# HGRN2 mixer on one Trainium2 core: values projected with positions on the partitions, two heads in a product of 256 columns

## The chip, the cores and the metric

The kernel runs on one core of a Trainium2 chip. The metric is the device time of one execution in microseconds, the median of the runs shown.

## The reference

Two layers of a decoder trunk on 1024 positions of width 1024. Layer 0 mixes with dilated window attention, layer 1 with HGRN2, a gated linear recurrence; each mixer is followed by a squared-ReLU MLP, and each sub-layer by a layer norm. The change is in layer 1's mixer, in short:

```python
q_raw, f_raw, i_raw = jnp.split(x @ w_in, [H * K, 2 * H * K], axis=-1)
log_f = jnp.logaddexp(jnp.log(lb), jnp.log1p(-lb) + jax.nn.log_sigmoid(z))
key = (1.0 - lb) * jax.nn.sigmoid(-z)
q = jax.nn.silu(q_raw); v = i_raw
b = jnp.cumsum(log_f, axis=3)                     # within chunks of 64 positions
q_dec, k_dec = q * jnp.exp(b), key * jnp.exp(-b)
a = jnp.where(causal, q_dec @ k_dec.T, 0.0)
kv = (key * jnp.exp(b_last - b)).T @ v            # per chunk, added up by a scan
o = a @ v + q_dec @ state                         # then RMS norm per head
return o @ w_out
```

There are 8 heads of width 128. The forget input f gives the keys (needs a chain of exponentials, logarithms and a running sum), q the queries, and i the values v, which no function is applied to.

## The kernel before, in words

Every fp32 product of the projections is made of three products in fp32r: each operand is split into a high part (a ScalarE copy, L146) and a low part (a VectorE subtraction, L147), and high x high, high x low and low x high are added up in PSUM. The input x lies transposed in SBUF, with its 1024 features on the partitions in 8 blocks, and the positions in two halves of 512 columns.

The mixer is `hgrn` (L1593). Its loop goes over 8 heads; each head has three projections (t = 1 forget, 0 query, 2 values) of two halves each, six slots. A slot is `proj` (L175 to L184): 24 products of 512 columns, weights stationary (128 x 128), positions moving, into one of three PSUM banks (`mm`), so the result has the head's 128 features on the partitions and positions as columns. ScalarE copies it out (L1755) to the tile ze (forget), qe (query) or vTh (values). After the second half of a forget or query projection `gate` (L1696) runs on all 1024 positions: L1703 to L1720 for the forget chain on ScalarE, VectorE and GpSimd (it makes the keys `kd`, L1716, in the tile called ls, and `kd2`, L1719, in ze), L1725 to L1731 for the query chain (`qd`, in qe). Head 0 is gated in halves, each right after its slot.

The rest of a head is cut into pieces (`head_pieces`, L1602) that are run behind the slots of the heads that follow, one list of pieces a slot (`pend`): first the transposes of the values (8 on TensorE and two ScalarE copies, L1605 to L1612, from vTh to vn, positions on the partitions), the scores (`amat`, L1615, products "as") and the transposes of the keys; then `kv(0)`; `omat(0)` and `kv(1)`; `omat(1)` (products "ho", L1645); nothing; and the output's transposes `otr` (L1675, products "opt"), each with a ScalarE copy to oN that multiplies by the norm's weight (L1680). The last head's pieces are left over and are given to the output projection `outproj_ln` (L932) as `fill`, which spreads them over its own products (`tick`, L964). Before the last slot `pre(oN)` loads and splits the first two tiles of the output weights (woh, wol) and of the heads' outputs (onr to hoh, hol).

SBUF tiles come from a pool of slots of 4 KB per partition (`U`, L102), PSUM from pools of banks (`bank`, L105: 3 mm, 2 s, 2 pt, 1 o). A scheduler that runs when the kernel is built fixes the order of the instructions on every engine from their readiness and the order of the program; on the chip each engine runs its own list in that order, and an instruction that waits holds up all that stand behind it. The weights of the next projections are loaded by SyncE (L152, 512 KB each) and split as a whole (128 x 1024).

Of the kernel before, what the change touches and what calls it, by code (L numbers as in the profile page):

```python
# [12 lines left out]
AF = mybir.ActivationFunctionType  # L13
# [47 lines left out]
       (30, 31, 33, 34, 35, 37, 39, 39, 40, 41, 41, 43, 43, 44))  # L61
STATS = ((13, 14, 16), (22, 23, 25))
# [6 lines left out]
def trunk_kernel(  # L69
# [6 lines left out]
    w_hgrn: bass.AP,  # L76
    w_hgrn_out: bass.AP,
# [1498 lines left out]
    class GateW:  # L1576


        def __init__(self):
            self.order = [(hd, t) for hd in range(8) for t in (1, 0, 2)]  # L1580
            self.loaded, self.raw = {}, None

        def ask(self):
            hd, t = self.order[0]
            self.raw = U("wr")
            nc.sync.dma_start(self.raw, w_hgrn[t * 8 + hd])

        def prefetch(self, i):
            if i < len(self.order) and i not in self.loaded:
                hd, t = self.order[i]  # L1590
                self.loaded[i] = w_load(w_hgrn[t * 8 + hd], "w", self.raw if i == 0 else None)

    def hgrn(xs, late, consts, pre, gw):  # L1593
# [6 lines left out]
        order, loaded, prefetch = gw.order, gw.loaded, gw.prefetch  # L1600

        def head_pieces(hd, kd, kd2, qd, vT, dec, oNt):  # L1602
            st = {}

            def trans(src, name):  # L1605
                d = U(name)
                for j in range(2):
                    pt = bank("pt", "hpt")
                    for i in range(4):
                        b = j * 4 + i  # L1610
                        nc.tensor.transpose(pt[:, i * P:(i + 1) * P], src[:, b * P:(b + 1) * P], ident)
                    act(d[:, j * 512:(j + 1) * 512], pt, AF.Copy)  # L1612
                st[name] = d

            def amat(j):  # L1615
                s = bank("s", "as")
                for i in range(4):
                    t = j * 4 + i
                    nc.tensor.matmul(s[:, i * P:(i + 1) * P], kd[:, t * P:(t + 1) * P], qd[:, t * P:(t + 1) * P],
                                     start=True, stop=True, skip_group_check=True)  # L1620
                nc.vector.copy_predicated(aTs[j], cm, s)

            def kv(j):
# [21 lines left out]
            def omat(j):  # L1645
                o = bank("o" if j == 0 else "s", "ho")
                for i in range(4):
# [27 lines left out]
            def otr(j):  # L1675
# [8 lines left out]
            amats = [lambda: amat(0), lambda: amat(1)]  # L1684
            keys = lambda: trans(kd2, "k2n")
            return [
                [lambda: trans(vT, "vn")] + (amats + [keys] if hd else [keys] + amats),
# [3 lines left out]
                [],  # L1691
# [41 lines left out]
        oN = []  # L1733
        pend = []
        prefetch(0)
        n = 0
        for hd in range(8):
            e = {}
            slots = [(t, h) for t in (1, 0, 2) for h in range(2)]
            if hd == 0:  # L1740
                slots = [(1, 1), (0, 1), (2, 1), (1, 0), (0, 0), (2, 0)]
                for i in range(3):
                    prefetch(i)
            seen = set()
            cur = {}
            for t, h in slots:
                bi = hd * 3 + (1, 0, 2).index(t)
                prefetch(bi)
                prefetch(bi + 1)
                if t not in e:  # L1750
                    e[t] = U(("qe", "ze", "vTh")[t])
                if bi == len(order) - 1 and h == 1 and hd:
                    pre(oN)
                o = proj(loaded[bi], xs[h])
                act(e[t][:, h * 512:(h + 1) * 512], o, AF.Copy)  # L1755
                both = (t, 1 - h) in seen
                seen.add((t, h))
                if pend:
                    for f in pend.pop(0):
                        f()  # L1760
                if late:
                    late.pop(0)()
                if hd == 0 or both:
                    gate(hd, t, e, cur, slice(h * 512, h * 512 + 512) if hd == 0 else slice(0, S))
            for i in range(3):
                del loaded[hd * 3 + i]
            oNt = U("oN")
            oN.append(ond[1, hd] if hd < SPILL[1] else oNt)
            new = head_pieces(hd, cur["kd"], cur["kd2"], cur["qd"], e[2], cur["dec"], oNt)
            if hd == 0:  # L1770
                new = [[]] + new
            pend = [(pend[i] if i < len(pend) else []) + (new[i] if i < len(new) else [])
                    for i in range(max(len(new), len(pend)))]
        return oN, pend
# [59 lines left out]
def _arrays(inputs):  # L1834
# [4 lines left out]
    def cols(w):  # L1839
# [10 lines left out]
        "w_hgrn": cols(i["hgrn_w_in"][0]),  # L1850
# [30 lines left out]
```

## Time and profile before

| | us |
|---|---|
| median of three runs | 2781.69 |
| lowest and highest run | 2781.52, 10449.96 |
| the profiled execution | 2781.63 |
| its span in the trace | 2779.8 |

The trace is of one execution. Its times count from the start of the span. A row of the timeline that ends in "x8" stands for eight instructions that follow one another; its length is from the first one's start to the last one's end. A product in plain fp32, as the scores, is run in two passes, so that eight of the program are sixteen in the trace. In brackets stands how long the engine was idle before a row, and which tile and line it waited for. "ScalarE" is ACT in the rows, "VectorE" DVE, "TensorE" PE, "SyncE" SP (SPq its DMA queue) and "GpSimd" POOL.

### The profile page before, as it was taken

What the parts mean: (1) busy time and instruction counts of PE and PEld (TensorE: products, weight loads), DVE (VectorE), ACT (ScalarE), POOL (GpSimd) and SP (SyncE); (2) the same over time, 40 slices, a digit from 0 to 9 for tenths busy, and PEclk for the clock granted to TensorE, in tenths of its full rate; (3) what the DMA queues carried; (4) which work ended last, traced back from release to release, by engine and by line L of the source; (5) the groups of instructions that cost most, each with busy time, mean ns of one, the idle gap of its engine ahead of it and who ended that gap; (6) DMA issues with size and microseconds to landing.
All of it is one profiled execution on the core that took longest, in us unless ns stands there. A gap on an engine that the chain in (4) does not pass through costs nothing. (4 is left out here: it accounts for less than half of the span.)

```text
span 2779.8 us, 40126 instructions
## 1 busy us (share of the span) xinstructions
PE 2755.9 (99%) x14312; PEld 2230.8 (80%) x14312; DVE 2081.6 (75%) x3880; ACT 1419.2 (51%) x3078; POOL 69.5 (3%) x46
## 2 busy tenths in 40 slices
PE   9999999999999999999999999999999999999998
PEld 7777777777777777888888888888888888888887
DVE  8768777777877779886686868475667887678687
ACT  5555555655555554544454435555553544454443
POOL 0000000000000001000000000110100100000000
PEclk9999999999999999999999999999999999999999
DMA  8766665756656623464493853011132365485654
GB/s 304 251 205 201 193 200 175 245 181 210 203 190 216 187 87 137 159 220 155 166 322 126 265 178 106 11 52 62 61 124 104 139 216 178 142 289 198 215 176 129
DMA packets 204040, 485.01 MB, mean 174 GB/s; under 512 B 28992, under 2 KB 42816, under 8 KB 203840
## 3 DMA queue, kind: packets, MB, share of 16 engines
q1 hardware_dynamic: 202640, 481.99, 51.8%
q8 instruction: 112, 1.84, 0.3%
q14 instruction: 88, 0.72, 0.1%
q10 hardware_dynamic: 1200, 0.46, 0.1%
HBM read 362.69 MB, written 94.11 MB: 164 GB/s over the span
## 5 line engine op out<-in xcount | busy, mean ns | idle before, releaser
L704 PE MATMUL pmm<-xh,H 128*128 128x512 f32 x1008 | 406.9, 404 | 1.4 <-ACT H L466 1.4
L706 PE MATMUL pmm<-xh,H 128*128 128x512 f32 x1008 | 394.4, 391 | 2.4 <-DVE H L474 2.3
L705 PE MATMUL pmm<-xl,H 128*128 128x512 f32 x1008 | 393.4, 390 | 0.9 <-DVE xl L147 0.9
L706 PEld LDWEIGHTS pmm<-xh,H 128*128 128x128 f32 x1008 | 189.2, 188 | 45.9 <-DVE H L474 4.5
L704 PEld LDWEIGHTS pmm<-xh,H 128*128 128x128 f32 x1008 | 189.5, 188 | 41.8 <-issue 3.6
L705 PEld LDWEIGHTS pmm<-xl,H 128*128 128x128 f32 x1008 | 189.8, 188 | 37.0 <-DVE xl L147 1.6
L550 ACT ACTIVATE p<-p,stats 128x128 f32<-128x128 f32 (+1 forms) x384 | 168.2, 440 | 92.3 <-DVE stats L547 92.0
L1355 PE MATMUL pdy<-dT,dS 128*128 128x512 f32 x512 | 199.2, 389 | 0.0
L1358 PE MATMUL pdy<-dT,dS 128*128 128x512 f32 x512 | 199.2, 389 | 0.0
L1359 PE MATMUL pdy<-dT,dS 128*128 128x512 f32 x512 | 199.2, 389 | 0.0
L547 DVE CUSTOM_DVE_ANT_0 p<-s,mask 128x128 f32<-128x128 f32 (+1 forms) x384 | 113.4, 348 | 71.6 <-PE s L536 60.9
L146 ACT ACTIVATE dS<-dr 128x512 fp32r<-128x512 f32 x192 | 119.5, 622 | 76.1 <-PE pdy L1359 34.9
L181 PE MATMUL pmm<-f0nh,wh 128*128 128x512 f32 x384 | 153.2, 399 | 0.0
L183 PE MATMUL pmm<-f0nh,wl 128*128 128x512 f32 x384 | 149.8, 390 | 0.0
L182 PE MATMUL pmm<-f0nl,wh 128*128 128x512 f32 x384 | 149.6, 390 | 0.0
L147 DVE TENSOR_TENSOR dS<-dr,dS 128x512 fp32r<-128x512 f32 x192 | 132.7, 691 | 13.4 <-ACT dS L146 13.3
L146 ACT ACTIVATE dT<-hold 128x512 fp32r<-128x512 f32 x128 | 80.0, 625 | 70.9 <-DVE hold L1334 30.5
L1165 ACT ACTIVATE H<-wc 128x512 fp32r<-128x512 f32 x128 | 77.2, 626 | 76.2 <-DVE wc L1158 48.2
L1358 PEld LDWEIGHTS pdy<-dT,dS 128*128 128x128 f32 x512 | 96.1, 188 | 20.1
L1355 PEld LDWEIGHTS pdy<-dT,dS 128*128 128x128 f32 x512 | 96.1, 188 | 20.0
L1359 PEld LDWEIGHTS pdy<-dT,dS 128*128 128x128 f32 x512 | 96.1, 188 | 19.7
L563 ACT ACTIVATE pts<-ppt 128x256 f32<-128x256 f32 (+1 forms) x192 | 84.6, 474 | 48.9 <-PE ppt L560 46.2
(405 smaller groups left out, 6850.3 us busy)
## 6 DMA issues: line engine op xcount, KB each, us to landing
xh<-xtd SPq DMA_DIRECT2D x110, 512.0 KB
xl<-xtd SPq DMA_DIRECT2D x110, 512.0 KB
dr<-hd SPq DMA_DIRECT2D x192, 256.0 KB
dr<-in_w_down_dram SPq DMA_DIRECT2D x128, 256.0 KB
rot<-e SPq DMA_DIRECT2D x192, 128.0 KB
wa<-in_w_up_dram SPq DMA_DIRECT2D x48, 512.0 KB
wb<-in_w_attn_dram SPq DMA_DIRECT2D x36, 512.0 KB
wa<-in_w_attn_dram SPq DMA_DIRECT2D x33, 512.0 KB
```

The lines of the kernel that those rows point to most:

```text
L146: act(hi, raw, AF.Copy)
L147: nc.vector.tensor_sub(lo, raw, hi.bitcast(F32))
L181: nc.tensor.matmul(o, wh[:, k], xs.h(k), start=k == 0, stop=False)
L182: nc.tensor.matmul(o, wh[:, k], xs.l(k), start=False, stop=False)
L183: nc.tensor.matmul(o, wl[:, k], xs.h(k), start=False, stop=k == NK - 1)
L550: act(p[:, h, :n], p[:, h, :n], AF.Exp, bias=sS[:, 0, h, b:b + 1], scale=-1.0, accum_out=sS[:, 1, h, b:b + 1])
L704: nc.tensor.matmul(o, wh, hi[k // 2][:, c], start=begin and k == 0, stop=False, skip_group_check=True)
L705: nc.tensor.matmul(o, wh, lo[k // 2][:, c], start=False, stop=False, skip_group_check=True)
L706: nc.tensor.matmul(o, wl, hi[k // 2][:, c], start=False, stop=end and k == 3, skip_group_check=True)
L1355: nc.tensor.matmul(o[q], h, T_[:, L], start=begin, stop=False, skip_group_check=True)
L1358: nc.tensor.matmul(o[q], h, T_[:, R], start=False, stop=False, skip_group_check=True)
L1359: nc.tensor.matmul(o[q], l, T_[:, L], start=False, stop=end, skip_group_check=True)
```

## The change

The heads are taken in pairs of 12 slots. Forget and query slots are as before. The values of two heads are projected together, with the roles of the operands exchanged: x is stationary (128 positions), and the weights of two heads, 256 columns, move (`values`). Such a slot makes two blocks of 128 positions, 48 products of 256 columns, and a pair has four of them. The result has positions on the partitions, as `kv` and `omat` want it, so the values are not transposed any more, and the pieces lose that step. The weights of the values come as a new input in this arrangement, in two tiles for each pair.

The order of the slots is now a table (`HORD`, one row for the first pair, one for the others), and so is the slot behind which each piece of the even and the odd head runs (`HPIECE`; 13 is the second slot of the next pair), the slots at which weights are asked for (`HASK`) and given free (`HFREE`). In the later pairs the order is: forget and query of the even head (four slots), three slots of values, forget of the odd head (first half), the last slot of values, query (first half), forget (second half), query (second half). Odd heads, and head 0, are gated in halves, the other even heads as a whole. The last slot of the mixer is thus the second query half of head 7, where before it was the second half of its values. `pre(oN)` is called after that slot's gate; seven lists of head 7's pieces go on to the output projection.

```diff
+HORD = (((1, 0, 1), (0, 0, 1), (2, 4), (1, 0, 0), (0, 0, 0), (2, 6), (2, 0), (2, 2),
+         (1, 1, 0), (0, 1, 0), (1, 1, 1), (0, 1, 1)),
...
+HPIECE = (((7, 8, 9, 10, 11, 12), (13, 14, 15, 16, 17, 18)),
...
-            self.order = [(hd, t) for hd in range(8) for t in (1, 0, 2)]
+            self.aps = []
+            for a in range(0, 8, 2):
+                self.aps += [w_hgrn[8 + a], w_hgrn[a], w_value[a // 2][:, 0:1024], w_value[a // 2][:, 1024:2048],
+                             w_hgrn[8 + a + 1], w_hgrn[a + 1]]
             self.loaded, self.raw = {}, None
...
-        def head_pieces(hd, kd, kd2, qd, vT, dec, oNt):
+        def head_pieces(hd, kd, kd2, qd, vn, dec, oNt):
...
-                                     st["vn"][r, t * P:(t + 1) * P], start=True, stop=True, skip_group_check=True)
+                                     vn(t)[r], start=True, stop=True, skip_group_check=True)
...
-                                         st["vn"][:, t * P:(t + 1) * P], start=True, stop=c == 0,
+                                         vn(t), start=True, stop=c == 0,
...
-            amats = [lambda: amat(0), lambda: amat(1)]
-            keys = lambda: trans(kd2, "k2n")
             return [
-                [lambda: trans(vT, "vn")] + (amats + [keys] if hd else [keys] + amats),
+                [lambda: trans("kd2", "k2n"), lambda: amat(0), lambda: amat(1)],
                 [lambda: kv(0)],
                 [lambda: omat(0), lambda: kv(1)],
                 [lambda: omat(1)],
-                [],
                 [lambda: otr(0)],
                 [lambda: otr(1)],
...
+        def values(n, t0):
+            o = bank("mm", "pmm")
+            w = [loaded[6 * n + 2 + i] for i in range(2)]
+            for i, t in enumerate((t0, t0 + 1)):
+                oc = o[:, i * 256:i * 256 + 256]
+                x_, c = xs[t // 4], slice((t % 4) * P, (t % 4) * P + P)
+                for k in range(NK):
+                    wh, wl = (half[:, (k % 4) * 256:(k % 4) * 256 + 256] for half in w[k // 4])
+                    nc.tensor.matmul(oc, x_.h(k, c), wh, start=k == 0, stop=False, skip_group_check=True)
+                    nc.tensor.matmul(oc, x_.h(k, c), wl, start=False, stop=False, skip_group_check=True)
+                    nc.tensor.matmul(oc, x_.l(k, c), wh, start=False, stop=k == NK - 1, skip_group_check=True)
+            if n not in vals:
+                vals[n] = [U("vn") for _ in range(2)]
+            act(vals[n][t0 // 4][:, (t0 % 4) * 256:(t0 % 4) * 256 + 512], o, AF.Copy)
+        oN, vals = [], {}
...
+        def gates(n, what):
+            if what[0] == 2:
+                return
+            t, b, h = what
+            hd = 2 * n + b
+            if hd == 0 or b:
+                gate(hd, t, *heads[hd], slice(h * 512, h * 512 + 512))
+            elif (hd, t, 1 - h) in done:
+                gate(hd, t, *heads[hd], slice(0, S))
...
+        for i in range(4):
+            prefetch(i)
+        for n in range(4):
+            for i, what in enumerate(HORD[n > 0]):
+                k = 12 * n + i
+                for m in (n - 1, n):
+                    for b in range(2):
+                        if m >= 0 and 12 * m + HPIECE[m > 0][b][0] == k:
+                            begin(m, b, [12 * m + a for a in HPIECE[m > 0][b]])
+                slot(n, what)
+                for j in HFREE[n > 0].get(i, ()):
+                    del loaded[6 * n + j]
+                while todo[k]:
+                    todo[k].pop(0)()
                 if late:
                     late.pop(0)()
+                gates(n, what)
+                if k == 47:
+                    pre(oN)
+                for j in HASK.get(i, ()):
+                    prefetch(6 * n + j)
+        begin(3, 1, [36 + a for a in HPIECE[1][1]])
+        return oN, todo[48:55]
...
-        "w_hgrn": cols(i["hgrn_w_in"][0]),
+        "w_hgrn": cols(i["hgrn_w_in"][0])[:16],
+        "w_value": i["hgrn_w_in"][0][:, 2 * D:].reshape(NK, P, 4, 2 * P).transpose(2, 1, 0, 3).reshape(4, P, NK * 2 * P),
```

On TensorE, at an even head's first pieces in the middle of the mixer, stood in the kernel before (pmm are projections, opt transposes of the output, hpt transposes of values (from vTh) or keys (from ze), as scores):

```order
L183 MATMUL pmm<-f0nh,wl 128x512
L1679 MATMUL opt<-ident,on 128x128 x4
L1611 MATMUL hpt<-ident,vTh 128x128 x8
L1619 MATMUL as<-qe,ls 128x128 x8
L1611 MATMUL hpt<-ident,ze 128x128 x8
L181 MATMUL pmm<-f0nh,wh 128x512
```

There now stands:

```order
L1749 MATMUL pmm<-wh,f0nh 128x256
L1750 MATMUL pmm<-wl,f0nh 128x256
L1751 MATMUL pmm<-wh,f0nl 128x256
L1690 MATMUL opt<-ident,on 128x128 x4
L1621 MATMUL hpt<-ident,ze 128x128 x8
L1630 MATMUL as<-qe,ls 128x128 x8
L190 MATMUL pmm<-f0nh,wh 128x512
```

The eight transposes from vTh are gone, the products ahead have 256 columns with x (f0nh, f0nl) as the stationary operand, and the transposes of the keys come before the scores.

On TensorE, at the end of the mixer, from the last projection's product to the output projection's first (pmm from woh and wol), stood:

```order
L183 MATMUL pmm<-f0nh,wl 128x512
L1679 MATMUL opt<-ident,on 128x128 x8
L1611 MATMUL hpt<-ident,vTh 128x128 x4
L1619 MATMUL as<-qe,ls 128x128 x8
L193 MATMUL pmm<-woh,hoh 128x512
L194 MATMUL pmm<-wol,hoh 128x512
```

There now stands (ho is `omat`):

```order
L192 MATMUL pmm<-f0nh,wl 128x512
L1690 MATMUL opt<-ident,on 128x128 x4
L1621 MATMUL hpt<-ident,ze 128x128
L1690 MATMUL opt<-ident,on 128x128 x4
L1621 MATMUL hpt<-ident,ze 128x128 x3
L1630 MATMUL as<-qe,ls 128x128 x4
L1663 MATMUL ho<-vn,aT 64x128 x2
L1621 MATMUL hpt<-ident,ze 128x128 x4
L1630 MATMUL as<-qe,ls 128x128 x4
L202 MATMUL pmm<-woh,hoh 128x512
L203 MATMUL pmm<-wol,hoh 128x512
```

Key transposes and scores of head 7's second half, which need both of its gates, now stand ahead of the output projection, which follows the last query slot directly.

On ScalarE, at the same place, stood (vTh are copies of the last two values' slots, the a tile is the query gate's work, woh and hoh are splits for the output projection):

```order
L1755 ACTIVATE vTh<-pmm 128x512
L1730 ACTIVATE a_18802<-a_18802 128x1024
L146 ACTIVATE woh<-wor 128x512 x2
L1755 ACTIVATE vTh<-pmm 128x512
L146 ACTIVATE woh<-wor 128x512 x2
L146 ACTIVATE hoh<-onr 128x512 x2
```

There now stands, from just behind the copy of the last query slot (a_18994, ls, ze and dec are steps of the forget gate, a_19135 of the query gate, oN copies of head 6's output):

```order
L1728 ACTIVATE dec<-a_18994 128x8
L1733 ACTIVATE a_19135<-qe 128x512
L1724 ACTIVATE ls<-ze,hc_C 128x512
L1734 ACTIVATE a_19135<-a_19135 128x512
L1691 ACTIVATE oN<-opt,hg 128x512
L1735 ACTIVATE a_19135<-a_19135,one 128x512
L1727 ACTIVATE ze<-ze,hc_C 128x512
L155 ACTIVATE woh<-wor 128x512 x2
L1738 ACTIVATE a_19135<-a_19135 128x512
L155 ACTIVATE woh<-wor 128x512
L155 ACTIVATE hoh<-onr 128x512 x2
```

The splits for the output projection now stand behind the steps of both gates of head 7's second half.

## Rows read from the trace of the kernel before

**Rows 1.** Page: the span, then each engine's busy time, share and instructions.

```profile
span 2779.8 us, 40126 instructions
...
PE 2755.9 (99%) x14312; PEld 2230.8 (80%) x14312; DVE 2081.6 (75%) x3880; ACT 1419.2 (51%) x3078; POOL 69.5 (3%) x46
```

**Rows 2.** Windows: the mixer's stage (stretch, its length, then the columns named).

```profile
core 0: us, PE busy (x) PEld busy (x) DVE busy (x) ACT busy (x) POOL busy (x), PEclk, DMA share, GB/s
1708.60:2053.60 345.00, 344.73 (x2116) 287.27 (x2115) 214.44 (x332) 192.32 (x287) 39.02 (x18) 1.00 0.18 62
```

**Rows 3.** Groups by line, 1708.6 to 2100: busy us, mean ns | idle before.

```profile
L181 PE MATMUL pmm<-f0nh,wh 128*128 128x512 f32 x384 | 153.2, 399 | 0.0
...
L1612 ACT ACTIVATE vn<-hpt 128x512 f32<-128x512 f32 x16 | 8.8, 602 | 0.3 <-PE hpt L1611 0.3
...
L1611 PE MATMUL hpt<-ident,vTh 128*128 128x128 f32 x64 | 8.7, 273 | 0.0
```

**Rows 4.** Timeline, TensorE, a projection: start us, length us, engine, line, operation.

```profile
1799.80 0.39 PE L181 MATMUL pmm<-f0nh,wh 128*128 128x512 f32 x1
...
1802.30 0.39 PE L183 MATMUL pmm<-f0nh,wl 128*128 128x512 f32 x1
```

**Rows 5.** Timeline, TensorE, head 0's transposes (hpt) and scores (as).

```profile
1754.38 1.03 PE L1611 MATMUL hpt<-ident,vTh 128*128 128x128 f32 x8
1755.25 0.39 PE L1619 MATMUL as<-qe,ls 128*128 128x128 f32 x2
1755.72 1.15 PE L1611 MATMUL hpt<-ident,ze 128*128 128x128 f32 x8
1756.70 1.73 PE L1619 MATMUL as<-qe,ls 128*128 128x128 f32 x14
```

**Rows 6.** Timeline, TensorE, attention: scores of 256 columns on 64 partitions.

```profile
303.34 1.14 PE L536 MATMUL s<-kT,qT 64*128 64x256 f32 x8
```

**Rows 7.** Timeline, SyncE's queue at the mixer's start.

```profile
1703.90 1.25 SPq L152 DMA_DIRECT2D wr<-in_w_hgrn_dram  x2
...
1715.65 2.44 SPq L152 DMA_DIRECT2D wr<-in_w_hgrn_dram  x4
```

**Rows 8.** Timeline, ScalarE, the first weight's split, and what it waited for.

```profile
1709.69 1.06 ACT L146 ACTIVATE wh<-wr 128x1024 fp32r<-128x1024 f32 x1 [2.66 <-DMA wr<-in_w_hgrn_dram]
```

**Rows 9.** Timeline, ScalarE, head 0's gates in halves (ze forget, qe query).

```profile
1732.91 0.59 ACT L1755 ACTIVATE ze<-pmm 128x512 f32<-128x512 f32 x1
...
1738.26 0.60 ACT L1755 ACTIVATE qe<-pmm 128x512 f32<-128x512 f32 x1 [0.40 <-PE pmm L183]
...
1746.51 0.71 ACT L1719 ACTIVATE ze<-ze,hc_C 128x512 f32<-128x512 f32 x1
```

**Rows 10.** Timeline, VectorE, the last step of that query gate.

```profile
1746.16 0.69 DVE L1731 TENSOR_TENSOR qe<-qe,a 128x512 f32<-128x512 f32 x1
```

**Rows 11.** Timeline, TensorE, the mixer's last two slots and its end.

```profile
2037.17 0.39 PE L183 MATMUL pmm<-f0nh,wl 128*128 128x512 f32 x1
...
2039.38 0.50 PE L181 MATMUL pmm<-f0nh,wh 128*128 128x512 f32 x1
...
2050.40 1.04 PE L1679 MATMUL opt<-ident,on 128*128 128x128 f32 x8
...
2053.42 0.48 PE L193 MATMUL pmm<-woh,hoh 128*128 128x512 f32 x1
...
2055.37 0.50 PE L195 MATMUL pmm<-woh,hol 128*128 128x512 f32 x1 [0.54 <-DVE hol L147]
```

**Rows 12.** Timeline, ScalarE, splits (woh, hoh) and output copies at that end.

```profile
2051.39 1.14 ACT L146 ACTIVATE woh<-wor 128x512 fp32r<-128x512 f32 x2
2052.44 1.14 ACT L146 ACTIVATE hoh<-onr 128x512 fp32r<-128x512 f32 x2
2053.47 1.25 ACT L1680 ACTIVATE oN<-opt,hg 128x512 f32<-128x512 f32 x2
```

**Rows 13.** Timeline, VectorE, the low part of the output projection's input.

```profile
2054.62 1.29 DVE L147 TENSOR_TENSOR hol<-onr,hoh 128x512 fp32r<-128x512 f32 x2
```

More of the change, by code (lines that the diff above doesn't have):

```diff
@@ L61 @@
        (30, 31, 33, 34, 35, 37, 39, 39, 40, 41, 41, 43, 43, 44))
+HORD = (((1, 0, 1), (0, 0, 1), (2, 4), (1, 0, 0), (0, 0, 0), (2, 6), (2, 0), (2, 2),
[3 rows of a table added]
+HPIECE = (((7, 8, 9, 10, 11, 12), (13, 14, 15, 16, 17, 18)),
+          ((6, 7, 9, 10, 11, 12), (13, 14, 15, 16, 17, 18)))
+HASK = {0: (2,), 1: (3,), 4: (4,), 6: (5,), 8: (6,), 10: (7,)}
+HFREE = ({3: (0,), 4: (1,), 7: (2, 3), 10: (4,), 11: (5,)}, {1: (0,), 3: (1,), 8: (2, 3), 10: (4,), 11: (5,)})
 STATS = ((13, 14, 16), (22, 23, 25))
@@ L76, in trunk_kernel @@
     w_hgrn: bass.AP,
+    w_value: bass.AP,
     w_hgrn_out: bass.AP,
@@ L1579, in __init__ @@
         def __init__(self):
-            self.order = [(hd, t) for hd in range(8) for t in (1, 0, 2)]
+            self.aps = []
+            for a in range(0, 8, 2):
+                self.aps += [w_hgrn[8 + a], w_hgrn[a], w_value[a // 2][:, 0:1024], w_value[a // 2][:, 1024:2048],
+                             w_hgrn[8 + a + 1], w_hgrn[a + 1]]
             self.loaded, self.raw = {}, None
         def ask(self):
-            hd, t = self.order[0]
             self.raw = U("wr")
-            nc.sync.dma_start(self.raw, w_hgrn[t * 8 + hd])
+            nc.sync.dma_start(self.raw, self.aps[0])
         def prefetch(self, i):
-            if i < len(self.order) and i not in self.loaded:
-                hd, t = self.order[i]
-                self.loaded[i] = w_load(w_hgrn[t * 8 + hd], "w", self.raw if i == 0 else None)
+            if i < len(self.aps) and i not in self.loaded:
+                self.loaded[i] = w_load(self.aps[i], "w", self.raw if i == 0 else None)
     def hgrn(xs, late, consts, pre, gw):
@@ L1599, in hgrn @@
         nc.sync.dma_start(sm, smask)
-        order, loaded, prefetch = gw.order, gw.loaded, gw.prefetch
-        def head_pieces(hd, kd, kd2, qd, vT, dec, oNt):
-            st = {}
+        loaded, prefetch = gw.loaded, gw.prefetch
+        def head_pieces(hd, kd, kd2, qd, vn, dec, oNt):
+            st = {"kd": kd, "kd2": kd2}
             def trans(src, name):
-                d = U(name)
+                d, src = U(name), st.pop(src)
                 for j in range(2):
@@ L1616, in amat @@
                 s = bank("s", "as")
+                kd = st["kd"] if j == 0 else st.pop("kd")
                 for i in range(4):
@@ L1731, in gate @@
                 nc.vector.tensor_mul(q, q, a3)
[L1733 to L1760, printed above, removed]
+        def values(n, t0):
[12 more added lines that the diff above has]
+            act(vals[n][t0 // 4][:, (t0 % 4) * 256:(t0 % 4) * 256 + 512], o, AF.Copy)
@@ new lines, in hgrn, with slot @@
+        oN, vals = [], {}
+        todo = [[] for _ in range(64)]
+        heads = [({}, {}) for _ in range(8)]
+        done = set()
+        def slot(n, what):
+            if what[0] == 2:
+                values(n, what[1])
+                return
+            t, b, h = what
+            hd = 2 * n + b
+            e, cur = heads[hd]
+            if t not in e:
+                e[t] = U(("qe", "ze")[t])
+            o = proj(loaded[6 * n + 4 * b + 1 - t], xs[h])
+            act(e[t][:, h * 512:(h + 1) * 512], o, AF.Copy)
+            done.add((hd, t, h))
@@ new lines, in gates, with begin, vn @@
+        def gates(n, what):
+            if what[0] == 2:
+                return
+            t, b, h = what
+            hd = 2 * n + b
+            if hd == 0 or b:
+                gate(hd, t, *heads[hd], slice(h * 512, h * 512 + 512))
+            elif (hd, t, 1 - h) in done:
+                gate(hd, t, *heads[hd], slice(0, S))
+        def begin(n, b, at):
+            hd = 2 * n + b
+            cur = heads[hd][1]
+            oNt = U("oN")
+            oN.append(ond[1, hd] if hd < SPILL[1] else oNt)
+            def vn(t):
+                return two[t // 4][:, (t % 4) * 256 + b * P:(t % 4) * 256 + b * P + P]
+            two = vals.pop(n) if b else vals[n]
+            heads[hd] = None
+            del cur["a"], cur["a3"]
+            for k, fs in zip(at, head_pieces(hd, cur["kd"], cur["kd2"], cur["qd"], vn, cur["dec"], oNt)):
+                todo[k] += fs
@@ L1761, in hgrn @@
                 if late:
                     late.pop(0)()
[L1763 to L1771, printed above, removed]
@@ L1772, in hgrn @@
-            pend = [(pend[i] if i < len(pend) else []) + (new[i] if i < len(new) else [])
-                    for i in range(max(len(new), len(pend)))]
-        return oN, pend
+                gates(n, what)
[5 more added lines that the diff above has]
+        return oN, todo[48:55]
     def rest(f, *args):
```

2 rows, old and new, of the table HORD are left out of this document.

## The prediction

> **What bounds the kernel now.** I read the page first: TensorE is busy for 2755.9 of 2779.8 us, VectorE for three quarters of it, ScalarE for half [rows 1]. So the time is TensorE's work plus the little that it waits, and the question is what the change does to both. Next I read the windows of the stage that is changed, layer 1's mixer: 344.73 of 345.00 us busy, at a granted clock of 1.00 (the upper of the two levels, 2.4 GHz), with VectorE at 214 and ScalarE at 192 us [rows 2]. Nothing there waits. A saving on ScalarE or VectorE is worth nothing in this stage; a microsecond less on TensorE is worth one, as long as no new wait appears. The groups by line say what TensorE does there: 384 products of 512 columns on each of three lines, of which a third is for the values, and 64 transposes of the values, with 16 copies on ScalarE behind them [rows 3]. A row's mean duration (399 ns) is no price, because products overlap. The price is the distance from one start to the next, read from the timeline: eleven distances in 2.50 us, 227.3 ns for a product of 512 columns [rows 4].
>
> **What it removes.** Eight transposes run from 1754.38 to 1755.25, 0.87 us; eight heads have eight each, so 8 x 0.87 = 7.0 us go. In that place of head 0, TensorE also stopped for the copies that empty the two transpose banks (the two "as" from 1755.25 take until 1755.72, though two cost 0.22), 0.25 us more [rows 5]. Total: -7.2. The 16 copies are 16 x 0.60 = 9.6 us of ScalarE [rows 3], which has 153 us free in the stage [rows 2]: nothing.
>
> **What it changes in the products.** The values' 384 products of 512 columns cost 384 x 0.2273 = 87.3 us. They become 768 of 256 columns, the same number of columns altogether. The stage has no row of 256 columns, so I bound the price. From below: eight products of 256 columns in attention (on 64 partitions, with the weights of 64) last 1.14 us from the first start to the last end, and if the last one takes 0.39 the distance is (1.14 - 0.39) / 7 = 107 ns [rows 6]; 768 x 107 = 82.2, a gain of 5.1. In the middle: half of 227.3 is 113.6, and nothing changes. From above, where the pipeline still works: 107 is what the columns take, so 512 take 214, and the remaining 13.6 ns belong to each product however short; then 120.6, 92.6 us, +5.3. A product of 128 columns with a load of 128 columns before it comes every 112 ns (fourteen scores last 1.73 us and two 0.39; the difference is twelve distances, 1.34 us) [rows 5], so a load of that size fits into 112 ns and is just hidden by 256 columns. I take 116 ns, between 112 and 120.6: 768 x 116 = 89.1, +1.8.
>
> The Trainium skill ("TensorE: Matmul & The Clock Gate", section "Back-to-back issue gap") puts a warm product at its columns over 2.4 plus 2.5 ns: 109.2 ns for 256 columns and 215.8 for 512, by which the term would be +1.0 by the page's own two figures; the trace does not bear out the second (227.3 ns [rows 4]). The Trainium skill (the same page, section "LDWEIGHTS (loading the stationary operand)") makes a load as long as its columns at half the column rate, 106.7 ns for 128 columns, about as long as the 256-column product that has to cover it; this speaks against the change, since the cover goes from twice the load to none to spare. The trace's 112 ns agree with it as a floor [rows 5], and the sum stays as it is.
>
> **What it moves.** First the start. The program now asks for four weight tiles instead of three before the first product. In before two are issued at 1703.90 and the rest from 1715.65, behind a store [rows 7]; a tile is split on ScalarE 5.8 us after its issue (1709.69 against 1703.90) [rows 8]. The fourth, the second half of the values' weights, goes behind the store, at 1715.65, and is split 5.8 us later, at 1721.5. The stage begins at about 1709; two slots of 24 x 0.2273 = 5.45 us, two groups of transposes of the stage before (1.7) and twelve products of the third slot (1.4) come before the first product that needs it: 1723. Cost 0, at most 1.
>
> Even heads keep their distance: their query gate has three slots (16 us) before the keys are transposed, as in before. Odd heads have less. Their last forget slot is the eleventh of twelve and their last query slot the twelfth; their keys and scores follow the second slot of the next pair. They are gated in halves, and a half chain is shown by head 0. Forget: from the copy at 1732.91 to the end of the last exponential at 1746.51 + 0.71 = 1747.22, 14.3 us. Query: from 1738.26 to 1746.16 + 0.69 = 1746.85 on VectorE, 8.6 us [rows 9, 10]. The forget half has three slots and some smaller products, 3 x 5.45 = 16.4, and the pieces of the even head between them (2.0 for output products, 8 transposes at 0.109), 19.3 us in all; the query half has two, 10.9 + 0.9 = 11.8 us. Both fit, the second by 3 us. Cost 0, up to 3 us for each of three odd heads.
>
> **The last odd head has no slots behind it.** In before the mixer ended with a values' product, and head 7's gates were under way for two slots before. TensorE went from the last product (2050.40) through transposes and scores into the output projection at 2053.42, and had to wait only 0.54 us, for the low part of its input at 2055.37, 4.97 us after the last product [rows 11]. Now the last slot is head 7's second query half, the slot before it the second forget half. Call the end of the last product T. The forget chain starts 0.4 us after its slot, which ends 5.45 us of products and one piece of output products (2037.17 to 2039.38, 2.2 us with the breaks [rows 11], less one product's 0.2) before T: T - 7.4 + 0.4 + 14.3 = T + 7.3. The query chain ends at T + 0.4 + 8.6 = T + 9.0, and in ScalarE's row there now stand among its steps two copies of the output (1.25 us for both) and two splits of the output's weights (1.14) [rows 12]; part of this falls into pauses of the chain, so I put it at T + 10.5. The order on TensorE has head 7's second four key transposes and four scores ahead of the first product of the output projection: it can start at T + 11. The split of its input (two copies, 1.14 us [rows 12]) now also stands behind the gate's exponential on ScalarE, and its low part on VectorE behind that (0.65 each [rows 13]): T + 12.5 to T + 13 for the product that waited at T + 4.97 before. TensorE's work up to there is 4.9 us (8 + 8 transposes at 0.109, 16 passes of scores at 0.112, five products at 0.23). So it waits 12.75 - 4.9 = 7.8 us, where it waited 0.54: +7, with bounds 3 (the pauses swallow all that is queued, and the first half's work fills more) and 10 (nothing overlaps). Behind the waiting scores stands the whole output projection, so nothing can be done meanwhile.
>
> **Sum.** -7.2 + 1.8 + 7 + 0 = +1.6 on the profiled execution's 2781.63, which is 1.8 above its span and 0.06 below the median of the runs, 2781.69. Forecast: 2783. A measurement of this kernel tells about 2%, 55.6 us, from no change.
>
> **Rivals.**
> A, the forecast: the gain of the transposes is real and is eaten by the wait at the mixer's end. For it: the two half chains of head 0 and the order of the rows. 2783.
> B: the wait at the end is hidden, since ScalarE and VectorE run emptier in that place than in head 0 (no splits of weights for another head), and the sum is -7.2 + 1.8 = -5.4: 2776. Against it: 11 us of chain can't shrink to 3; at least half of the 7 remains unless the steps run much faster than in head 0 [rows 9].
> C: odd heads are late in each pair. The query half has only 3 us to spare, and in ScalarE's order steps of both gates, copies and splits of two 1024-column weight tiles (1.05 us each) stand between. If each of three pairs loses 3 us: 2783 + 9 = 2792.
> D, slower: the load of the weights is not hidden behind 256 columns. Each product then costs its load and its columns one after the other, 112 + 113.6 = 226 ns, as long as a whole one of 512: 768 x 0.226 = 173.6, +86.3, and with the other terms 2783 - 1.8 + 86.3 = 2867. It decides (2%) from 2837, that is 54 / 768 = 70 ns more per product, 186 ns. For it: 112 ns for load and 128 columns is barely less than 113.6. Against it: in attention products of 256 columns, with loads of their own, come every 107 ns [rows 6].
>
> **How the numbers follow.** A 0.60, B 0.23, C 0.11, D 0.03, and 0.03 for what I don't see. The range goes from 2772 (B with the lower price of the products, 2776 - 4, rounded) to 2795 (C, and the upper price): it leaves out D and the unseen. A, B and C are all within 2%: same 0.95. Slower is D and one of the unseen 0.03, 0.04; faster 0.01.
>
> **What would show it.** In the changed kernel's timeline, the distance between two products of 256 columns: 107 to 121 ns is right, 200 is D. No rows of transposes of the values. In the waits of TensorE after the last projection's product: an idle time of 5 to 9 us ended by VectorE (the query's product) or by the split of the output's input; less than 2 us is B. In the windows of the mixer: TensorE idle below 1 us in the interior, else C. The forecast is wrong if the mixer's stage shrinks by over 8 us, or if products of 256 columns take over 130 ns.

## The result and the profile after

The median of five runs is 2795.6 us (2794.7 to 2797.56), that of the kernel before 2782.0. The ratio is 1.005, with a 95% interval from 1.0034 to 1.0066: half a per cent slower, 0.6 us above the forecast's range and 12.6 above its number. The profiled execution took 2797.56 us.

The page of the changed kernel (columns as in [rows 1]):

```profile
span 2795.8 us, 40855 instructions
...
PE 2758.0 (99%) x14632; PEld 2247.6 (80%) x14632; DVE 2073.8 (74%) x3912; ACT 1421.3 (51%) x3114; POOL 73.3 (3%) x54
```

TensorE is busy for only 2.1 us more than before, and the span is 16.0 us longer. So most of the loss is not work. Its two stages, the mixer and the start of the output projection (columns as in [rows 2]):

```profile
1710.50:2062.00 351.50, 341.94 (x2413) 299.94 (x2412) 200.85 (x356) 188.04 (x310) 40.31 (x24) 0.99 0.17 56
2062.00:2114.00 52.00, 46.29 (x270) 37.58 (x269) 35.95 (x73) 25.25 (x50) 2.54 (x2) 0.93 0.37 116
```

The mixer, which had 0.27 us of idle time in 345, now has 9.56 in 351.5, the stretch behind it 5.7, and in both the granted clock is below 1.00 on average. Who waited for whom, TensorE from 1700 to 2130 (us in total, times, longest):

```profile
engine line waited for: us in total, times, longest us
PE ho L1663 <- DVE stB L1650: 9.6, 4, 3.2
PE as L1630 <- DVE qe L1739: 2.6, 1, 2.6
PE ho L1663 <- ACT oN L1691: 2.1, 1, 2.1
PE hpt L1621 <- ACT ze L1727: 0.8, 1, 0.8
PE pmm L204 <- DVE hol L156: 0.3, 1, 0.3
```

The first line is new and stands in the middle of the mixer: four times the output products of `omat(1)` waited for the state scan. The next four are the end of the mixer. By stretches, read from the starts of products in both timelines:

| stretch | before | after | difference |
|---|---|---|---|
| start of the first projection product | 1709.07 | 1710.50 | +1.4 |
| from there to the start of the last projection product | 341.10 | 351.43 | +10.3 |
| from there to the output projection's last product | 107.33 | 111.60 | +4.3 |
| from there to the last product of the kernel | 613.83 | 613.71 | -0.1 |

The first line is not the change's: among the kernels of this study the stage begins between 1708.80 and 1711.89, and up to there TensorE runs the same products. Of the 1.4 us, 1.2 are there already 60 us after the start of the span, behind a stretch of the changed kernel from 39.0 to 42.4 us at a granted clock of 0.50 that the kernel before does not have.

**The products.** Two rows of the timeline of the changed kernel, in a slot of values (start, length):

```profile
1944.08 0.28 PE L1749 MATMUL pmm<-wh,f0nh 128*128 128x256 f32 x1
...
1945.52 0.28 PE L1749 MATMUL pmm<-wh,f0nh 128*128 128x256 f32 x1
```

Twelve distances in 1.44 us: 120.0 ns for a product of 256 columns, against 227.3 for one of 512 [rows 4]. There are no transposes of values any more.

**The wait in the middle.** VectorE's row around the wait that ends at 1966.08, in the third pair (L1673 is the reduction for the norm of the even head's first half, L1650 the scan of the states, L1736 and L1739 steps of the odd head's query gate, L156 a split of weights):

```profile
1956.24 0.69 DVE L1726 TENSOR_TENSOR ze<-a,ze 128x512 f32<-128x512 f32 x1 [1.91 <-ACT ls L1724]
1959.40 0.69 DVE L1673 TENSOR_REDUCE rms<-sq 128x4 f32<-128x512 f32 x1 [2.46 <-ACT sq L1671]
1960.00 0.34 DVE L1650 SCALAR_TENSOR_TENSOR stB<-stB,dec,kvps 128x128 f32<-128x128 f32 x1
...
1960.33 0.69 DVE L1736 SCALAR_TENSOR_TENSOR a<-qe,a 128x512 f32<-128x512 f32 x1
...
1961.01 0.34 DVE L1650 SCALAR_TENSOR_TENSOR stB<-stB,dec,kvps 128x128 f32<-128x128 f32 x1
...
1962.75 0.35 DVE L1650 SCALAR_TENSOR_TENSOR stB<-stB,dec,kvps 128x128 f32<-128x128 f32 x1
...
1963.09 1.22 DVE L156 TENSOR_TENSOR wl<-wr,wh 128x1024 fp32r<-128x1024 f32 x1
...
1965.08 0.68 DVE L1739 TENSOR_TENSOR qe<-qe,a 128x512 f32<-128x512 f32 x1
1965.68 0.72 DVE L1650 SCALAR_TENSOR_TENSOR stB<-stB,dec,kvps 128x128 f32<-128x128 f32 x2
```

The last products of the state (kvps) had ended at 1957.0. The scan's first step on stB runs at 1960.00, because the reduction stands ahead of it in VectorE's row, and that waited 2.46 us for the squares (sq) from ScalarE. So VectorE stood idle from 1956.93 to 1959.40, with the scan's input there from 1957.0. On ScalarE the squares stood behind steps of the odd head's half gates, though TensorE had finished their input at 1955.9:

```profile
1957.60 0.62 ACT L1733 ACTIVATE a<-qe 128x512 f32<-128x512 f32 x1
1958.25 0.63 ACT L1734 ACTIVATE a<-a 128x512 f32<-128x512 f32 x1
1958.78 0.58 ACT L1671 ACTIVATE sq<-ho 128x512 f32<-128x512 f32 x1
```

Then the scan's seven steps take until 1966.4, with two steps of the query gate, a weight split of 1.22 us and the norm between them. TensorE's last product of the slot ended at 1962.91. In the kernel before the same rows on VectorE were these:

```profile
2031.47 0.69 DVE L1662 TENSOR_REDUCE rms<-sq 128x4 f32<-128x512 f32 x1 [2.76 <-ACT sq L1660]
2032.07 0.34 DVE L1639 SCALAR_TENSOR_TENSOR stB<-stB,dec,kvps 128x128 f32<-128x128 f32 x1
...
2034.82 1.11 DVE L1639 SCALAR_TENSOR_TENSOR stB<-stB,dec,kvps 128x128 f32<-128x128 f32 x3
...
2037.14 0.34 DVE L1639 SCALAR_TENSOR_TENSOR stB<-stB,dec,kvps 128x128 f32<-128x128 f32 x1
```

There the reduction came 0.7 us after its input, the scan took 5.4 us, and its last step ended at 2037.48; `omat(1)` began at 2037.49. But what `omat(1)` waits for is not the last step. In the changed kernel it began at 1966.08, when the sixth of the seven steps had just ended (1966.03) and the seventh was still running (until 1966.40), and so it is at all four waits. In the kernel before, the sixth step (the third of the row "x3") ended at 2035.93: `omat(1)` had 1.5 us of slack. In the changed kernel the scan starts 3.0 us behind the last products of the state, against 0.2 before, and takes 6.0 us to the end of its sixth step, against 3.9. Of these 4.9 us, 1.5 go into the slack and 0.2 into a slot that is that much longer; the other 3.2 are the wait.

**The clock.** Windows of the changed kernel around two of these waits (columns as in [rows 2]):

```profile
1872.00:1878.00 6.00, 4.99 (x35) 4.44 (x36) 2.51 (x6) 1.20 (x2) 0.00 (x0) 0.50 0.00 0
...
1960.00:1966.00 6.00, 2.91 (x13) 2.07 (x11) 6.00 (x16) 4.46 (x8) 1.30 (x1) 1.00 0.00 0
1966.00:1972.00 6.00, 5.92 (x50) 5.04 (x51) 3.20 (x9) 2.46 (x6) 0.00 (x0) 1.00 0.00 0
```

In the wait of 3.17 us from 1869.84 the granted clock falls to 0.50, 1.2 GHz, and it stays there until about 1878.8; products of 512 columns start every 427 ns in that stretch. In the wait of the same length in the third pair, and after it, it stays at 1.00.

**The end.** TensorE's rows from the last projection's product to the output projection (to be read beside [rows 11]):

```profile
2062.16 0.60 PE L1690 MATMUL opt<-ident,on 128*128 128x128 f32 x4
...
2066.60 0.44 PE L1663 MATMUL ho<-vn,aT 128*64 128x128 f32 x4 [2.08 <-ACT oN L1691]
2067.82 0.66 PE L1621 MATMUL hpt<-ident,ze 128*128 128x128 f32 x4 [0.79 <-ACT ze L1727]
2071.03 2.07 PE L1630 MATMUL as<-qe,ls 128*128 128x128 f32 x8 [2.56 <-DVE qe L1739]
2072.76 0.77 PE L202 MATMUL pmm<-woh,hoh 128*128 128x512 f32 x1
```

The chain of waits is nearly the forecast one: a copy of the output behind gate steps on ScalarE (2.08), the forget gate's key (0.79), the query gate (2.56). The forecast had the copies as a delay of the query gate, not as a wait of their own. The output projection starts 10.6 us after the last projection's product, at the lower clock.

### The profile page after: what moved, and what is told of

It reads as the page before. It is cut to its first block, busy times and chain, and to the rows that moved or that the text cites. A ratio compares the mean times of both kernels' runs of the same rounds, so it can differ in the third digit from the quotient of the medians.

```text
span 2795.8 us, 40855 instructions
## 1 busy us (share of the span) xinstructions
PE 2758.0 (99%) x14632; PEld 2247.6 (80%) x14632; DVE 2073.8 (74%) x3912; ACT 1421.3 (51%) x3114; POOL 73.3 (3%) x54
## 5 line engine op out<-in xcount | busy, mean ns | idle before, releaser
L156 DVE TENSOR_TENSOR dS<-dr,dS 128x512 fp32r<-128x512 f32 x192 | 131.1, 683 | 13.7 <-ACT dS L155 13.7
L190 PE MATMUL pmm<-f0nh,wh 128*128 128x512 f32 x256 | 102.3, 400 | 0.0
L191 PE MATMUL pmm<-f0nl,wh 128*128 128x512 f32 x256 | 100.6, 393 | 0.0
L192 PE MATMUL pmm<-f0nh,wl 128*128 128x512 f32 x256 | 100.4, 392 | 0.0
```

Source lines behind the costliest of these rows:

```text
L156: nc.vector.tensor_sub(lo, raw, hi.bitcast(F32))
```

## The experiments

The theory after the result: the waits before `omat(1)` come from the order of VectorE's row, where the scan stands behind a reduction that waits for ScalarE, and ScalarE is behind with half gates. The rivals: the half gates' load as such; another resource. Each run is compared with runs of the kernel before on the same chip. Unless said otherwise, an edit is made to the changed kernel.

**e1_swap: states ahead of the first half's output.**

```diff
-                [lambda: omat(0), lambda: kv(1)],
+                [lambda: kv(1), lambda: omat(0)],
```

> State products (kv(1)) are issued ahead of the first half's output products (omat(0)) in each head's third list; nothing else. Theory 1 (four waits of 9.6 us before the even heads' omat(1) come from VectorE's row, where the state scan stands behind the RMS reduction, which itself waits for ScalarE behind the odd head's half gates): the scan can start about 3 us earlier, each wait falls below 1.2 us, 9.6 us become 3 or less, and the fall of the clock behind the second of them is gone: about 2786. Rival (the scan is late because of the sum of the half gates' steps on VectorE, wherever they stand): the waits stay above 6 us together, 2792 to 2796.

2784.19 us, ratio to the kernel before 1.0007 (0.9997 to 1.0016): 11.4 less than the changed kernel. All four waits are gone, and no window of the mixer has a clock below 1.00. VectorE in the same place:

```profile
1947.47 0.69 DVE L1726 TENSOR_TENSOR ze<-a,ze 128x512 f32<-128x512 f32 x1 [1.91 <-ACT ls L1724]
1948.08 1.49 DVE L1650 SCALAR_TENSOR_TENSOR stB<-stB,dec,kvps 128x128 f32<-128x128 f32 x4
...
1951.77 0.68 DVE L1673 TENSOR_REDUCE rms<-sq 128x4 f32<-128x512 f32 x1
1952.36 0.33 DVE L1650 SCALAR_TENSOR_TENSOR stB<-stB,dec,kvps 128x128 f32<-128x128 f32 x1
...
1954.33 0.34 DVE L1650 SCALAR_TENSOR_TENSOR stB<-stB,dec,kvps 128x128 f32<-128x128 f32 x1
```

The scan's four first steps run at 1948.08 in one piece, 3.7 us ahead of the reduction. The sixth step ends at 1952.69, and `omat(1)` follows at 1953.82: 1.1 us early, where it was 3.2 us late. Of these 4.3 us, 1.9 are the states' products themselves, which now run ahead of 1.9 us of output products on TensorE; by that alone 1.3 us of each of the two long waits would have been left. The rest comes with the order on VectorE. The mixer takes 338.42 us, 2.7 less than before the change. The theory holds, and the rival of sheer load falls.

**e2_late: `omat(1)` one slot later.**

```diff
-          ((6, 7, 9, 10, 11, 12), (13, 14, 15, 16, 17, 18)))
+          ((6, 7, 9, 11, 11, 12), (13, 14, 15, 16, 17, 18)))
```

(The first pair's row likewise.)

> The even heads' omat(1) runs one slot later (behind the twelfth slot of a pair instead of the eleventh). Theory 1: the scan ends at the same time, TensorE has one more slot (5.45 us) in between, all four waits are gone, and with them the stretch at the lower clock behind the second: minus 9.3 and minus 2.7, about 2783.5; the wait at the mixer's end stays. Rival (TensorE is late there for another reason, such as the bank that the products are written to): the waits move along with omat(1).

2797.35 us, ratio 1.0054 (1.0039 to 1.0069). A miss. The wait for the scan is gone, but another has taken its place:

```profile
PE opt L1690 <- DVE on L1682: 12.5, 4, 4.4
PE hpt L1621 <- ACT ze L1727: 3.1, 1, 3.1
```

The output's transposes (opt) of the same half now wait for the normed output (L1682): I had moved the reader of the scan and left the reader of the norm where it was, one slot behind. Whether the row is late only once per half, or too full altogether, the next run had to tell.

**e12_late_both: that reader one slot later too.** On top of e2_late (and the first pair's row likewise):

```diff
-          ((6, 7, 9, 11, 11, 12), (13, 14, 15, 16, 17, 18)))
+          ((6, 7, 9, 11, 11, 13), (13, 14, 15, 16, 17, 18)))
```

> The second run's kernel with the even heads' last output transposes one slot later as well (the second slot of the next pair), so that the norm of their second half has as long as in the changed kernel, plus the time that VectorE's row took from it. If the second run's waits only moved from the scan's reader to the norm's reader, as its profile shows, both are now covered: less than 2 us of waits ahead of the mixer's last slot, and with the end's waits (5 to 6 us) 2784 to 2786. If VectorE's row is simply too full in that stretch: the wait moves on to the next reader (the odd head's scores) and stays above 6 us, 2790 or more.

2783.57 us, ratio 1.0004 (0.9995 to 1.0014). The only waits left are the two of the mixer's end:

```profile
PE hpt L1621 <- ACT ze L1727: 3.1, 1, 3.1
PE opt L1690 <- DVE on L1682: 2.2, 1, 2.2
```

So the lateness is of some 3 us, once in each pair, and more distance cures it as well as a better order does.

**e3_whole: heads 1, 3 and 5 gated as a whole.**

```diff
-            if hd == 0 or b:
+            if hd in (0, 7):
```

> Heads 1, 3 and 5 are gated as a whole again; head 7 and head 0 in halves. Theory 1: the waits before omat(1) of heads 0, 2 and 4 (7.9 us) fall below 1.5 together, since no half gate stands in VectorE's row there; but heads 1, 3 and 5 now come late: a whole forget gate takes 24 us and has 19.3, so their transposes and scores wait 4 to 6 us each, with stretches at the lower clock behind: 2800 to 2808. Rival (the half gates don't cause the waits before omat(1)): these stay at 7 us or more.

2809.77 us, ratio 1.0097 (1.008 to 1.0114). Two of its waits:

```profile
PE hpt L1621 <- ACT ze L1727: 15.1, 4, 4.8
...
PE ho L1663 <- DVE stB L1650: 1.6, 1, 1.6
```

The waits for the scan are down to one (1.6, in the last pair, whose odd head still has half gates) and three of 0.2 to 0.4; heads 1, 3 and 5 wait 4.8 us each for their keys. Both sides of the theory hold: the half gates make the wait in the middle, and without them the odd heads come late. The time is a little above the range I gave, 2800 to 2808, since the clock falls to 0.50 behind each of these three waits.

**e7_halves: half gates alone, in the kernel before.**

```diff
-                if hd == 0 or both:
-                    gate(hd, t, e, cur, slice(h * 512, h * 512 + 512) if hd == 0 else slice(0, S))
+                if hd % 2 or hd == 0 or both:
+                    gate(hd, t, e, cur, slice(h * 512, h * 512 + 512) if hd % 2 or hd == 0 else slice(0, S))
```

> The kernel before, with one part of the change alone: heads 1, 3, 5 and 7 gated in halves, in the old order of slots, values transposed as before. If half gates by themselves delay the state scan: waits before omat(1) of the even heads of 0.5 to 2 us each, 2784 to 2790. If it takes the new order too: no waits over 0.3 us, 2782 within 1.

2793.48 us, ratio 1.004 (1.0024 to 1.0055). Half gates alone cost 11 us, more than I had put, in the old order of slots and with nothing else changed. The waits make 8.8 of it, and behind the longest, 4.3 us, the granted clock is 0.50 from 1783.6 to 1790.4:

```profile
PE ho L1652 <- DVE stB L1639: 8.8, 4, 4.3
```

**e10_halves_states: the same with the states ahead** (the edit of e1_swap on top).

> The seventh run's kernel (the kernel before with odd heads gated in halves) with the states ahead of the first half's output. If the order of scan and RMS reduction on VectorE is the cause in the old order of slots too: its 8.8 us of waits fall below 2, 2782 to 2784. If the half gates' load is: they stay above 5, 2788 or more.

2781.24 us, ratio 0.9997 (0.9988 to 1.0007). Of the 8.8 us one wait of 1.6 in the first pair of heads is left. That the time is the one of the kernel before has two halves, though: the mixer takes 342.50 us, 1.4 more than before, and the stretch behind it 104.75, 2.6 less, since the swapped order also takes breaks out of head 7's states and output products in the output projection (2.5 us). So half gates cost 1.4 us here, and nothing but that one wait where the states come first. The swap alone in the kernel before was not run; by this run it would be worth up to some 2.6 us there.

**e8_cut: products of 256 columns alone, in the kernel before.** The values' products are cut into two, weights stationary as before.

```diff
+        for c in (slice(0, 256), slice(256, 512)):
+            for k in range(NK):
+                nc.tensor.matmul(o[:, c], wh[:, k], xs.h(k, c), start=k == 0, stop=False, skip_group_check=True)
...
-                o = proj(loaded[bi], xs[h])
+                o = (proj2 if t == 2 else proj)(loaded[bi], xs[h])
```

> The kernel before, with the values' products of 512 columns cut into two of 256 each, weights still stationary, results and transposes as before. If the 120 ns of a 256-column product are its columns and some 13.5 ns that each product costs whatever its length: the same 120 ns, 768 x (120.0 - 113.65) = plus 4.9, 2787. If they come from x being the stationary operand or from its loads out of other tiles: 113.6 to 115 ns, 2782 to 2783.

2786.74 us, ratio 1.0018 (1.0009 to 1.0027). Its timeline:

```profile
1824.61 0.28 PE L192 MATMUL pmm<-f0nh,wh 128*128 128x256 f32 x1
...
1825.69 0.28 PE L192 MATMUL pmm<-f0nh,wh 128*128 128x256 f32 x1
```

Nine distances in 1.08 us, 120.0 ns again. The price goes with the length of the product, not with the operand that stands still.

**e4_tail: the last pair's values last.** A third row of the tables for the last pair; `omat(0)` and `kv(1)` get entries of their own.

```diff
+        ((1, 0, 0), (1, 0, 1), (0, 0, 0), (0, 0, 1), (2, 0), (2, 2), (1, 1, 0), (1, 1, 1), (0, 1, 0), (0, 1, 1),
+         (2, 4), (2, 6)))
...
+          ((6, 7, 8, 11, 12, 10, 13), (13, 14, 15, 15, 16, 17, 18)))
```

> In the last pair the odd head's four forget and query slots come ahead of the last two slots of values, so that values' products end the mixer; head 6's second half follows in the output projection. My forecast's term for the end (+7, of which the profile shows 5.7 us of waits and some 3 us by the lower clock): both fall to under 1.5 us together, and so does the last pair's wait before omat(1), 1.6: about 2786. Rival (the output projection then waits for head 6's states, scan and output in the same place): 3 us or more of waits stay there, 2789 to 2793.

2790.42 us, ratio 1.0028 (1.0018 to 1.0038). The end's waits fall to 0.64, and the stretch behind the mixer from 111.6 to 107.1. Three waits for the scan remain (7.9), and the odd head's weights, needed a slot earlier, come late twice (2.1 us with the wait for ScalarE's part). With that, and with an end that gained 4.5 us and not the 7 or more that I had put, the time is 4 us above my expectation.

**e9_pre: on top of e1_swap, `pre(oN)` ahead of the last slot.**

```diff
+                if k == 47:
+                    pre(oN)
                 slot(n, what)
...
-                if k == 47:
-                    pre(oN)
```

> The first run's kernel (states ahead), with the output projection's first loads and splits asked for before the last query slot, as in the kernel before, instead of behind its gate. If the waits at the mixer's end (6.1 us there) are the gate chains of head 7 themselves: they stay within 1 us, 2783.5 to 2784.5. If the splits and copies in ScalarE's row among the gates make them, as my forecast's 1.5 us said: 1 to 2 us less, 2782 to 2783.

2778.37 us, ratio 0.9988 (0.9978 to 0.9997), 5.8 less than e1_swap: more than either theory gave. TensorE at its end:

```profile
2047.92 0.48 PE L202 MATMUL pmm<-woh,hoh 128*128 128x512 f32 x1
...
2052.36 0.39 PE L204 MATMUL pmm<-woh,hol 128*128 128x512 f32 x1
2052.59 0.60 PE L1621 MATMUL hpt<-ident,ze 128*128 128x128 f32 x4
...
2055.57 0.66 PE L1621 MATMUL hpt<-ident,ze 128*128 128x128 f32 x4 [1.71 <-ACT ze L1727]
2056.09 0.50 PE L202 MATMUL pmm<-woh,hoh 128*128 128x512 f32 x1
```

The gate chains are not faster: the forget gate's last step (L1727) ends at 2055.5 here and at 2054.65 in e1_swap. But eighteen products of the output projection, whose inputs are now split in time, stand ahead of the keys and scores, from 2047.92 to 2052.6. Of 6.1 us of waits 2.3 are left, the longest 1.7, and the clock stays at 1.00.

**e5_both and e6_ask: states ahead and values last; then the last pair's odd weights asked for earlier.**

```diff
-                for j in HASK.get(i, ()):
+                for j in (HASK if n < 3 else {0: (2,), 1: (3,), 3: (4,), 5: (5,)}).get(i, ()):
```

> The edits of the first and the fourth run together: states ahead of the first half's output, and the last pair's values last. By their sum, from the first run's 2784.2: minus 4.5 for the end, plus up to 2.1 for the odd head's weight splits, which are now needed a slot earlier: 2780 to 2782. Rival (the two waits hide behind each other and only one gain is to be had): 2784 or more.

> As the run before, with the last pair's odd weights asked for one slot earlier. If the waits for weight splits (2.1 us in the fourth run) came from the asking: they fall below 0.7 us and the time to 2779 to 2780.5, faster than the kernel before by about 0.1%. If they came from VectorE's row, they stay and the time is that of the run before.

e5_both took 2780.18 us, ratio 0.9992 (0.9983 to 1.0001): the gains add up. e6_ask took 2776.99, ratio 0.9982 (0.9974 to 0.9991), a little better than I had put; its only wait of the stretch is

```profile
PE pmm L208 <- DVE hol L160: 0.6, 1, 0.6
```

**e11_ask_pre: e6_ask with `pre(oN)` ahead of the last slot.**

> The sixth run's kernel with the output projection's first loads and splits asked for before the last slot. The sixth run's end waits only 0.7 us, so at most that is to be had: 2776 to 2777, the same as the sixth run; if the early splits push into ScalarE's and VectorE's row ahead of head 7's last gate steps and these come late: 2778 to 2780.

2776.75 us, ratio 0.9981 (0.9972 to 0.999): as e6_ask. These two beat both kernels, by 0.2% and 0.7%. How much of the 0.2% the kernel before would have from the swapped order alone is open (e10_halves_states).

## Why the prediction was wrong

The sign of the forecast was right and its size was not: +1.6 forecast, +13.6 between medians. By its terms, with the distances between starts added up by operation:

- **The transposes, -7.2: right.** Transposes of values and keys took 11.90 us in the mixer before and 6.11 after, 1.91 and 1.09 behind it: -6.6. The scores, which no longer stop for the transpose banks, save 0.8.
- **The products, +1.8: mis-sized.** I took 116 ns and measured 120.0; e1_swap, which has no waits in the mixer, shows +5.0 for all projections together. The upper price that I had worked out, 120.6, was the right one, and its reason fits: what a product of 512 takes beyond its columns belongs to the product. e8_cut shows the price by itself. The Trainium skill ("TensorE: Matmul & The Clock Gate", section "Back-to-back issue gap") has 262 cycles for 256 columns at 2.4 GHz, an estimate of 109.2 ns, as the gap of products by themselves. The 120.0 measured here, with a load for each product, decide. Rival D is out: the loads are hidden.
- **The start, 0: right.** No wait stands there.
- **"Even heads keep their distance", and with it the interior of the mixer at a cost of 0: this step failed.** I compared distances from a head's gates to its own keys. I did not ask what the odd head's half gates do to the other instructions in ScalarE's and VectorE's rows at the time, the even head's squares, reduction and scan. The row for that was at hand: `omat(1)` followed the slot's last product at once [rows 11], and VectorE's row shows that the scan left it 1.5 us to spare, against the 4.9 by which the scan came later. The waits cost 9.6 and the lower clock behind one of them 3.0 (1.3 on the projections' products, 1.7 on the output products), for which the sum had no term; another 0.4 are short breaks in the odd heads' output products. Without this term the mixer comes to 5.0 - 5.8 - 1.6 (scores, output products and output transposes) - 0.3 (the idle time of before) = -2.7, which is what e1_swap measures.
- Rival C's sign, more than 1 us of idle time in the mixer's interior, came true with 9.56, and C had the right kind of mechanism, queues on ScalarE and VectorE, at the wrong place: I looked for the odd heads' own lateness. That they are on time is right; e3_whole shows that they would not be without half gates.
- **The end, +7: right in its waits, too large in sum.** The waits grew by 5.2, and scores and output projection, in part at the lower clock, took 2.9 more; but the transposes of the values (0.8, counted above), the states (1.6) and the output products (1.3) took 3.8 less, with fewer breaks between them: +4.3. (The 4.9 us of TensorE's work in my sum are 4.7 by its own terms, which changes little.) One sentence was wrong: "nothing can be done meanwhile". e9_pre shows that it is not the gates that keep TensorE idle, but that the output projection's splits were issued behind them. The order of ScalarE's row, my +1.5, was not what the gain came from: the gate chain ended no earlier.

So the gain of the transposes exists: in e1_swap the mixer is 2.7 us shorter, 7.2 and more saved, 5.0 given back to the shorter products. It was covered by two waits, each of which a change of order removes.

## What to carry to other kernels

When a change splits work on an engine that isn't the bottleneck into smaller steps, list what stands between them in that engine's row, and find for each of these the reader on the bottleneck and its slack; an instruction that does not wait may have little of it, here 1.5 us. Which step a reader waits for is seen where it does wait: here the sixth of seven. Where a long scan and a short reduction become ready together, issue the one first whose reader comes first, since an in-order row makes the scan wait for whatever the reduction waits for. Before calling a wait at the end of a stage unavoidable, look whether the next stage's products could run in it, and what keeps their inputs back. Halving the columns of a product cost the same small amount for each product more in both arrangements here: 768 x 6.4 ns.

## What the runs showed of the hardware

A product in fp32r with its own load comes every 227.3 ns for 512 columns [rows 4] and every 120.0 for 256, and for 256 in either arrangement of the operands (the changed kernel, e8_cut). That is 107.3 ns for 256 columns more; if the price goes in a straight line, which two lengths don't show, 12.7 ns of each product do not depend on its length. The granted clock fell to 0.50 in one wait of 3.17 us and not in another of the same length in the same place of the next pair; where it fell, products of 512 columns started every 427 ns until 5 to 6 us after TensorE went on. In e4_tail it fell just behind both of these waits. Why in the one and not in the other was not settled.
